# A two-layer decoder trunk on one core: preparing a pair's first blocks earlier, and the order of copies and casts at a turn of runs

## The chip, the cores and the metric

The kernel runs on one core of one Trainium2 chip. The metric is the device time of one execution in microseconds, as the median of three runs. The engines are TensorE (PE in the profile, with its weight loads as PEld), VectorE (DVE), ScalarE (ACT), GpSimd (POOL) and SyncE (SP), which issues the weight loads from memory.

## The reference

Two layers over 256 positions, model width 2048, feed-forward width 8192. Each layer is a mixer (a gated short convolution in the first layer, latent attention in the second) and a squared-ReLU MLP, each followed by a layer norm of 2^0.5 times the input plus the result:

```python
def sq_relu_mlp(x, w1, w2):
    return jnp.square(jax.nn.relu(x @ w1)) @ w2

for layer in range(DEPTH):            # DEPTH = 2
    mix = short_conv_mixer(...) if layer < N_A else mla_mixer(...)
    h = layer_norm(ALPHA * h + mix, ln_g[layer, 0], ln_b[layer, 0])
    h = layer_norm(ALPHA * h + sq_relu_mlp(h, mlp_w1[layer], mlp_w2[layer]),
                   ln_g[layer, 1], ln_b[layer, 1])
```

All of it is in float32. The change touches the two MLPs only.

## The kernel before

**Precision.** A float32 product is made of several products of a reduced format. Every weight block is split into a high part and a remainder: `split` (L144, L145) casts on ScalarE (`hi`) and subtracts on VectorE (`lo = raw - hi`). TensorE then multiplies high by high, low by high and high by low.

**The stream of weights.** All weights are read in the order of use, in a list `stream` of entries. An entry of kind "unit" is 128x1024 elements, one raw load (L165), one cast and one subtraction. A chunk of W1 (128 columns of the hidden layer) is two units. An entry of kind "plain" or "fast" is a *pair*: the rows of W2 for 256 hidden columns and 1024 output columns (one of two blocks, b = 0 or 1), two raw loads.

**Pairs.** A plain pair is multiplied with eight block products (`PLAINS`), 24 matmuls of 512 columns. A fast pair goes by the Strassen-Winograd scheme with seven (`FAST`), 21 matmuls: each of seven forms adds the product of a combination of the activations (`forms`, L665 to L668) and one of the weights to one of seven running sums in PSUM, numbered 1 to 7. The weight combinations are made from the raw blocks in place. `prepare` does it in three steps, with a `yield` between:

1. load both raw tiles; split the first (`hi`, `lo`: blocks 11 and 22); three subtractions in place (L193), of which each needs the one before;
2. split the result (`hi_t`, `lo_t`: combinations T1 and T2); a fourth subtraction; split that (the half-size `t`: T4);
3. split the second raw tile (`hi`, `lo`: block 21 and T3).

A plain pair has two steps, a unit one. Split blocks live in a pool of eight buffers (`WA`), raw tiles in one of six (`RAW`), T4 in one.

**Runs and turns.** `plan` lays out the MLP: runs of four pairs, alternately of block 0 and of block 1, with one W1 chunk after nearly every pair, so that TensorE works by turns on a chunk (L230, L234: `mm_like`) and on a group of seven or eight products (L295 to L297: `dot`). Runs of block 1 begin with a plain pair, the rest is fast; seven fast pairs and a plain one make a period. Only one block's sums fit into PSUM. At the end of a run (`turn`) ScalarE copies each sum out to SBUF (`spill`, L584) and the other block's sum back in (`seed`, L588), in the order of `FAST` or of the plain forms.

**Other work in the stage.** A finished chunk is evacuated by `whole` (L336 on ScalarE, L337 on VectorE). After every second one come ReLU (L722) and square (L658) on ScalarE, the activation forms on VectorE, and a split of the result (`hc`, `ha`). At the end of the runs `fold` (L614) and `combine` (L626, L627) turn the sums into the result.

**What sets the order.** The program is recorded in the order of the Python calls, and a scheduler then fixes the order on each engine at build time, by this order as priority and a cost model of its own; it also hands out the pools' buffers. On the chip each engine works through its list in that order. How early weights are prepared is set by `take`, which is called when a chunk or a group needs its entry: it first runs `prepare` steps up to eight steps past the start of that entry (`WA`), across the whole list in order of the stream.

Of the kernel before, what the change touches and what calls it, by code (L numbers as in the profile page):

```python
# [31 lines left out]
RAW, WA = 6, 8  # L32
# [7 lines left out]
GROUP = 3  # L40
# [8 lines left out]
def trunk(ctx: ExitStack, tc: tile.TileContext, xT, vecs, w_in, w_out, w_kv, w_q, w_uk, w_uv,  # L49
# [26 lines left out]
    stream = []  # L76
# [34 lines left out]
    size = {"unit": 1, "plain": 2, "fast": 3}  # L111
    start = [0]
# [3 lines left out]
    class Banks:  # L116
# [15 lines left out]
        @classmethod  # L132
        def next(cls):
            cls.count += 1
            if cls.only is not None:
                return cls.only
            return cls.more if cls.more is not None and cls.count % 8 >= 4 else pmm

    state = {"made": 0, "next": 0}
    ready = {}  # L140

    def split(hi, lo, src):

        nc.scalar.copy(hi, src)  # L144
        nc.vector.tensor_tensor(lo, src, hi.bitcast(F32), ALU.subtract)  # L145

    def tiled(w):
        return w.rearrange("p (b c) -> p b c", c=P)

    def parts(i):  # L150
        return tuple(whl.tile([P, 8, P], F32R, tag=t, name=f"{t}{i}") for t in ("hi", "lo"))
# [11 lines left out]
    def load_raw(i, src):  # L163
        raw = raws.tile([P, 1024], F32, tag="raw", name=f"raw{i}")
        nc.sync.dma_start(raw, src)  # L165
        return raw

    def prepare(i):

        kind, *src = stream[i]  # L170
        if kind == "unit":
            raw = load_raw(i, src[0])
            hi, lo = ready[i] = parts(i)
            split(hi, lo, tiled(raw))
            yield
            return
        r1, r2 = (load_raw(f"{i}_{j}", v) for j, v in enumerate(src))

        def finished(r, name):
            w = parts(f"{i}_{name}")  # L180
            split(*w, tiled(r))
            return [[v.rearrange("p b c -> p (b c)")[:, o:o + BW] for v in w] for o in (0, BW)]

        b11, b22, b21, b12 = r1[:, :BW], r1[:, BW:], r2[:, :BW], r2[:, BW:]
        out = {}
        if kind == "plain":
            out["11"], out["22"] = finished(r1, 1)
            yield
            out["21"], out["12"] = finished(r2, 2)
            ready[i] = out  # L190
            yield
            return
        minus = lambda o, x, y: nc.vector.tensor_tensor(o, x, y, ALU.subtract)  # L193
        out["11"], out["22"] = finished(r1, 1)
        minus(b11, b12, b11)
        minus(b12, b12, b22)
        minus(b22, b22, b11)
        yield
        out["T1"], out["T2"] = finished(r1, "t")
        minus(b11, b21, b22)  # L200
        f = state["fast"].tile([P, 2, BW], F32R, tag="t4", name=f"t4_{i}", bufs=1)
        split(f[:, 0, :], f[:, 1, :], b11)
        out["T4"] = [f[:, 0, :], f[:, 1, :]]
        yield
        out["21"], out["T3"] = finished(r2, 2)
        ready[i] = out
        yield

    def all_steps():
        for i in range(2 * GROUP, len(stream)):  # L210
            yield from prepare(i)

    making = all_steps()

    def take(n=2):

        i = state["next"]
        state["next"] += n
        while state["made"] < min(start[i] + WA, start[-1]):
            next(making)  # L220
            state["made"] += 1
        got = [ready.pop(i + j) for j in range(n)]
        return got

    def psum(name):
        return Banks.next().tile([P, 512], F32, tag="mm", name=name)
# [18 lines left out]
    def mm_like(ps, w, x, n=NC):  # L245

        for h in range(0, NC, n):
            for k in range(h, h + n):
                high(ps, w, k, x[k], k == 0)
            for k in range(h, h + n):  # L250
                low(ps, w, k, x[k], k == NC - 1)
# [22 lines left out]
    def group_of(n):  # L274

        return [(take(), psum("ps_g")) for _ in range(n)]

    def products(n, x, group=0, cuts=()):

        ws = group_of(group)  # L280
        at = [0, *cuts, NC]
        for k0, k1 in zip(at, at[1:]):
            if ws:
                mm_run(ws, x, k0, k1, NC, tiles_first=True)
        yield from [ps for _, ps in ws]
        for i in range(group, n):
            w = take()
            ps = psum("ps_u")
            mm_like(ps, w, x)
            yield ps  # L290
# [42 lines left out]
    def whole(ps, out):  # L333

        t = tmp.tile([P, T], F32, tag="evac", name="t")
        nc.scalar.copy(t, ps[:, T:])  # L336
        nc.vector.tensor_tensor(out, ps[:, :T], t, ALU.add)  # L337
# [174 lines left out]
    for half, cuts in enumerate(FIRST):  # L512
        pieces = [load(2 * u + half, first[:, GROUP * half + u, :], cuts) for u in range(GROUP)]
        for b0, b1 in zip(cuts, cuts[1:]):
            at = slice(8 * half + b0, 8 * half + b1)
# [4 lines left out]
                put_split(xhl[m], xres[:, m, :])  # L520
            for p in pieces:
                next(p)
    state["made"] = 2 * GROUP
    nc.sync.dma_start(vec, vecs)

    zt = array("b", F32R, "z", NC, 2 * T)
# [4 lines left out]
    for m in range(NC):  # L531
# [17 lines left out]
        if m >= NC // 2:  # L549
# [4 lines left out]
    summed(ln, products(NC, z), residual)  # L554

    FAST = (("1", "11", "11"), ("3", "S4", "22"), ("5", "S1", "T1"), ("6", "S2", "T2"),
            ("4", "22", "T4"), ("2", "12", "21"), ("7", "S3", "T3"))
    PLAINS = (("3", "12", "22"), ("1", "22", "22"), ("2", "11", "11"), ("4", "21", "11"),
              ("3", "11", "12"), ("1", "21", "12"), ("2", "12", "21"), ("4", "22", "21"))

# [77 lines left out]
    def mlp(idx, ln, hook, blocks, fast):  # L638
# [8 lines left out]
        def normal():  # L647
            k = next(todo, None)
            if k is not None:
                ln.normal(k, xhl[k])  # L650
# [3 lines left out]
        def pair():  # L654
            return fast.tile([P, 8 * P], F32, tag="sf", name="sf", bufs=2)

        def square(f):
            nc.scalar.activation(f[:, :4 * P], f[:, :4 * P], AF.Square)  # L658

        def forms(f):  # L660

            a21, a11, a12 = (f[:, i * P:(i + 1) * P] for i in (1, 0, 2))
            s1, s2, s4 = (f[:, i * P:(i + 1) * P] for i in (4, 6, 7))
            blocks = f.rearrange("p (a c) -> p a c", c=P)
            nc.vector.tensor_tensor(s1, a21, f[:, 3 * P:4 * P], ALU.add)  # L665
            nc.vector.tensor_tensor(blocks[:, 5:7, :], blocks[:, 1:5:3, :], a11.unsqueeze(1).to_broadcast([P, 2, P]),
                                    ALU.subtract)
            nc.vector.tensor_tensor(s4, a12, s2, ALU.subtract)  # L668
# [31 lines left out]
        def parts_of(j):  # L700

            i = j % 4
            if j >= 4:
                both = [(one[:, i, c * P:(c + 1) * P], two[:, i, c * P:(c + 1) * P]) for c in range(8)]
            else:
                both = [[t[:, i, (4 * o + c) * P:(4 * o + c + 1) * P] for o in range(2)] for t in (one, two) for c in range(4)]
            return dict(zip(NAMES, both))
# [4 lines left out]
        for at, step in enumerate(steps):  # L712
            if step[0] == "m":
                m = step[1]
                w, ps = take(), psum("ps_m")
                mm_like(ps, w, xhl, 8)
                if m % 2 == 0:
                    f = pair()
                half = f[:, m % 2 * T:(m % 2 + 1) * T]
                whole(ps, half)  # L720
                if m % 2:
                    nc.scalar.activation(f[:, :4 * P], f[:, :4 * P], AF.Relu)  # L722
                    square(f)
                    j, cols = m // 2, 4 * P
                    if j < KEPT:
                        forms(f)
                        cols = 8 * P
                    split(one[:, j % 4, :cols], two[:, j % 4, :cols], f[:, :cols])
                if m == FF // P - 3:
                    Banks.only = None  # L730
                continue
            _, b, j, plain, first, last = step
            w, = take(1)
            later = [s for s in steps[at + 1:] if s[0] == "group"]
            turns = plain and bool(later) and not later[0][3]
            sums.group(b, w, parts_of(j), plain, last, turns)
            if later:
                if last:
                    sums.turn(later[0][1], later[0][3])
                elif turns:  # L740
                    sums.spill("1")
                    sums.seed("1", (b, "1"))
            if first and j + 4 >= KEPT and b == 0 and j + 2 >= KEPT:
                folded = sums.fold(1)
            if not later:
                folded = sums.combine(0) + folded
            if count < 4:
                normal()
                normal()
            if hook is not None:  # L750
                hook(count)
            count += 1
# [37 lines left out]
    with tc.tile_pool(name="fast1", bufs=1) as fast:  # L790
        mlp(1, before, prepare_one, to_wide, fast)
# [250 lines left out]
    with tc.tile_pool(name="fast2", bufs=1) as fast:  # L1042
        mlp(3, after, None, to_out, fast)
# [86 lines left out]
```

## Time and profile before

| | |
|---|---|
| median of three runs | 2031.51 us (2030.67 to 2031.93) |
| the profiled execution | 2031.37 us |
| its span, first to last instruction | 2029.6 us |
| TensorE busy, matmuls | 2004.9 us (99%) |
| VectorE busy | 1729.8 us (85%) |
| ScalarE busy | 1384.2 us (68%) |
| DMA | 385.31 MB, 190 GB/s on average |
| granted TensorE clock | 0.999 |

The first copy of a sum (L584) starts at 423.5 us of the span, in the first layer's MLP, the last at 1935.3, in the second's; between the two MLPs lies the attention. Matmuls overlap one another, so the shown length of one is more than the time from one to the next: the busy share says that TensorE hardly rests, not how fast it works. In a row of groups the columns are line, engine, operation, tile written and tiles read, shapes, count, busy us, mean ns, idle us before them and what ended it. In a timeline a row has its start and length in us, and in brackets the idle time before it and what ended that.

### The profile page before, as it was taken

What the parts mean: (1) busy time and instruction counts of PE and PEld (TensorE: products, weight loads), DVE (VectorE), ACT (ScalarE), POOL (GpSimd) and SP (SyncE); (2) the same over time, 40 slices, a digit from 0 to 9 for tenths busy, and PEclk for the clock granted to TensorE, in tenths of its full rate; (3) what the DMA queues carried; (4) which work ended last, traced back from release to release, by engine and by line L of the source; (5) the groups of instructions that cost most, each with busy time, mean ns of one, the idle gap of its engine ahead of it and who ended that gap; (6) DMA issues with size and microseconds to landing.
All of it is one profiled execution on the core that took longest, in us unless ns stands there. A gap on an engine that the chain in (4) does not pass through costs nothing.

```text
span 2029.6 us, 29846 instructions
## 1 busy us (share of the span) xinstructions
PE 2004.9 (99%) x11088; PEld 1735.4 (86%) x11088; DVE 1729.8 (85%) x2575; ACT 1384.2 (68%) x2071; POOL 2.3 (0%) x21
## 2 busy tenths in 40 slices
PE   9999999999999999999999999999999999999997
PEld 8888888988888888888889998898888888888886
DVE  7667677799999999999988888779899999999996
ACT  6444445577877888777756655568777788787861
POOL 0000000000000000000000000000000000000000
PEclk9999999999999999999999999999999999999999
DMA  9665556455555565555654534655555556556672
GB/s 312 206 190 190 189 189 189 150 183 194 180 207 179 205 207 198 203 174 207 235 189 157 167 124 131 201 168 166 187 189 199 193 207 208 182 196 203 207 231 102
DMA packets 108002, 385.31 MB, mean 190 GB/s; under 512 B 11984, under 2 KB 13392, under 8 KB 107856
## 3 DMA queue, kind: packets, MB, share of 16 engines
q1 hardware_dynamic: 107712, 383.13, 56.6%
q8 instruction: 87, 1.43, 0.3%
q14 instruction: 59, 0.48, 0.1%
q10 hardware_dynamic: 144, 0.26, 0.0%
HBM read 381.25 MB, written 2.10 MB: 189 GB/s over the span
## 4 chain that ended last, share of the span: by engine, by line
PE 61%; DVE 17%; ACT 14%; issue 5%; DMA 2%; DVEq 0%; ACTq 0%; SPq 0%
PE ps_u L230 13%; PE ps_m L230 9%; PE ps_u L234 7%; DVE lo L145 7%; PE ps_m L234 5%; DVE raw L193 4%; ACT hi L144 4%; PE sum L296 3%; PE sum L297 3%; PE sum L295 3%; ACT sums L584 2%; ACT hi_t L144 2%; DVE lo_t L145 2%; ACT sum L588 2%; DMA raw<-in_w_dram 1%
## 5 line engine op out<-in xcount | busy, mean ns | idle before, releaser
L145 DVE TENSOR_TENSOR lo<-raw,hi 128x1024 fp32r<-128x1024 f32 x712 | 850.7, 1219 | 127.8 <-ACT hi L144 51.2
L144 ACT CAST hi<-raw 128x1024 fp32r<-128x1024 f32 x712 | 726.2, 1050 | 261.2 <-PE ps_u L230 158.1
L230 PE MATMUL ps_m<-xhl,hi 128*128 128x512 f32 x1792 | 449.3, 391 | 3.0 <-DVE sf L337 2.2
L230 PEld LDWEIGHTS ps_m<-xhl,hi 128*128 128x128 f32 x1792 | 328.6, 188 | 69.1 <-DVE sf L337 2.8
L234 PEld LDWEIGHTS ps_m<-xhl,lo 128*128 128x128 f32 x1792 | 244.3, 190 | 17.4
L234 PE MATMUL ps_m<-xhl,lo 128*128 128x256 f32 x1792 | 249.7, 282 | 0.0
L296 PE MATMUL sum<-lo,hc 128*128 128x512 f32 x512 | 202.9, 396 | 1.0 <-DVE lo L145 1.0
L295 PE MATMUL sum<-hi,hc 128*128 128x512 f32 x512 | 196.8, 396 | 5.2 <-ACT sum L588 5.1
L193 DVE TENSOR_TENSOR raw<-raw,raw 128x512 f32<-128x512 f32 x276 | 189.3, 686 | 3.0
L297 PE MATMUL sum<-hi,ha 128*128 128x512 f32 x448 | 175.1, 391 | 0.0
L144 ACT CAST hi_t<-raw 128x1024 fp32r<-128x1024 f32 x92 | 96.6, 1050 | 113.5 <-DVE raw L193 113.4
L230 PE MATMUL ps_u<-xhl_a,hi 128*128 128x512 f32 x720 | 172.0, 391 | 0.0
L145 DVE TENSOR_TENSOR lo_t<-raw,hi_t 128x1024 fp32r<-128x1024 f32 x92 | 112.7, 1225 | 68.5 <-ACT hi_t L144 68.5
L230 PEld LDWEIGHTS ps_u<-xhl_a,hi 128*128 128x128 f32 x720 | 132.4, 188 | 25.8
L584 ACT COPY sums<-sum 128x512 f32<-128x512 f32 x204 | 118.0, 583 | 43.3 <-PE sum L297 41.4
L295 PEld LDWEIGHTS sum<-hi,hc 128*128 128x128 f32 x512 | 95.6, 188 | 31.5 <-ACT sum L588 9.4
L296 PEld LDWEIGHTS sum<-lo,hc 128*128 128x128 f32 x512 | 96.5, 189 | 23.5 <-DVE lo L145 8.4
L588 ACT COPY sum<-sums 128x512 f32<-128x512 f32 x186 | 110.0, 593 | 2.7
L297 PEld LDWEIGHTS sum<-hi,ha 128*128 128x128 f32 x448 | 84.3, 188 | 15.9
L234 PEld LDWEIGHTS ps_u<-xhl_a,lo 128*128 128x128 f32 x720 | 92.3, 191 | 3.5
L234 PE MATMUL ps_u<-xhl_a,lo 128*128 128x256 f32 x720 | 93.4, 283 | 0.0
L722 ACT ACTIVATE sf<-sf 128x512 f32<-128x512 f32 x56 | 35.4, 631 | 57.2 <-DVE sf L337 57.2
(240 smaller groups left out, 3285.0 us busy)
## 6 DMA issues: line engine op xcount, KB each, us to landing
raw<-in_w_dram SPq DMA_DIRECT2D x288, 512.0 KB, 4.5
raw<-in_w2f_dram SPq DMA_DIRECT2D x224, 512.0 KB, 5.7
raw<-in_w_in_dram SPq DMA_DIRECT2D x90, 512.0 KB, 4.3
raw<-in_w_out_dram SPq DMA_DIRECT2D x32, 512.0 KB, 4.1
raw<-in_w_o_dram SPq DMA_DIRECT2D x32, 512.0 KB, 3.9
raw<-in_w_kv_dram SPq DMA_DIRECT2D x10, 512.0 KB, 4.3
raw<-in_w_q_dram SPq DMA_DIRECT2D x8, 512.0 KB, 4.0
raw<-in_w_uk_dram SPq DMA_DIRECT2D x8, 512.0 KB, 4.2
```

The source lines that it names most:

```text
L144: nc.scalar.copy(hi, src)
L145: nc.vector.tensor_tensor(lo, src, hi.bitcast(F32), ALU.subtract)
L193: minus = lambda o, x, y: nc.vector.tensor_tensor(o, x, y, ALU.subtract)
L230: nc.tensor.matmul(ps, w[blk // 8][0][:, blk % 8, :], x, start=first, stop=False)
L234: nc.tensor.matmul(ps[:, :T], w[blk // 8][1][:, blk % 8, :], x[:, :T], start=False, stop=last)
L295: nc.tensor.matmul(ps, x[0], w[0], start=first, stop=False, skip_group_check=goes_on)
L296: nc.tensor.matmul(ps, x[0], w[1], start=False, stop=False, skip_group_check=goes_on)
L297: nc.tensor.matmul(ps, x[1], w[0], start=False, stop=last, skip_group_check=goes_on)
L584: nc.scalar.copy(self.slot(self.live.pop(p)), self.bank[p])
L588: nc.scalar.copy(self.bank[p], self.at(key))
L722: nc.scalar.activation(f[:, :4 * P], f[:, :4 * P], AF.Relu)
```

## The change

Two things are moved; the amount of work stays the same.

First, the order in which entries are prepared is now a list of its own (`sequence`). Where two units (a W1 chunk) are followed by a fast pair, the pair's first step is put in front of the two units and its other steps behind them: pair, unit, unit, pair, pair. `make_up_to` works through this list with one generator per entry. The second and third step of a fast pair are divided differently: the second tile's split (21, T3) moves ahead of T4's, and T4 goes into the third step. The order of the forms is changed to match: the form that uses T4 (number 4) is now the last of the seven, in `group` as in `turn`.

Second, `take` has a second argument, how many steps to run ahead, and the last group of a run asks for five instead of eight. The steps that this leaves out are recorded after the turn, so behind the copies of the sums.

```diff
+        yield
+        out["21"], out["T3"] = finished(r2, 2)
         f = state["fast"].tile([P, 2, BW], F32R, tag="t4", name=f"t4_{i}", bufs=1)
         split(f[:, 0, :], f[:, 1, :], b11)
         out["T4"] = [f[:, 0, :], f[:, 1, :]]
-        yield
-        out["21"], out["T3"] = finished(r2, 2)
         ready[i] = out
         yield
 
-    def all_steps():
-        for i in range(2 * GROUP, len(stream)):
-            yield from prepare(i)
-
-    making = all_steps()
-
-    def take(n=2):
+    sequence, i = [], 2 * GROUP
+    while i < len(stream):
+        if [k for k, *_ in stream[i:i + 3]] == ["unit", "unit", "fast"]:
+            sequence += [i + 2, i, i + 1, i + 2, i + 2]
+            i += 3
+        else:
+            sequence += [i] * size[stream[i][0]]
+            i += 1
+    making = {}
+    last = {i: at for at, i in enumerate(sequence)}
+
+    def make_up_to(n):
+        while state["made"] < min(n, len(sequence)):
+            i = sequence[state["made"]]
+            state["made"] += 1
+            if i not in making:
+                making[i] = prepare(i)
+            next(making[i])
+
+    def take(n=2, ahead=None):
         i = state["next"]
         state["next"] += n
-        while state["made"] < min(start[i] + WA, start[-1]):
-            next(making)
-            state["made"] += 1
-        got = [ready.pop(i + j) for j in range(n)]
-        return got
+        mine = max(last.get(j, -1) + 1 for j in range(i, i + n))
+        make_up_to(max(mine, start[i] - 2 * GROUP + (WA if ahead is None else ahead)))
+        return [ready.pop(i + j) for j in range(n)]
...
     FAST = (("1", "11", "11"), ("3", "S4", "22"), ("5", "S1", "T1"), ("6", "S2", "T2"),
-            ("4", "22", "T4"), ("2", "12", "21"), ("7", "S3", "T3"))
+            ("2", "12", "21"), ("7", "S3", "T3"), ("4", "22", "T4"))
...
             _, b, j, plain, first, last = step
-            w, = take(1)
+            w, = take(1, 5 if last else None)
```

More of the change, by code (lines that the diff above doesn't have):

```diff
@@ L522, in trunk @@
                 next(p)
-    state["made"] = 2 * GROUP
     nc.sync.dma_start(vec, vecs)
```

## The prediction

> **What bounds the kernel.** I read the page's busy times first, then TensorE's groups of instructions, then the waits, then the timelines of TensorE, ScalarE and VectorE round one turn of runs. The page:
>
> ```profile
> span 2029.6 us, 29846 instructions
> PE 2004.9 (99%) x11088; PEld 1735.4 (86%) x11088; DVE 1729.8 (85%) x2575; ACT 1384.2 (68%) x2071; POOL 2.3 (0%) x21
> ```
>
> TensorE is shown busy for 99%, so the change can win only what TensorE waits. Its groups (count, busy us, mean ns, idle before) and one row of the waits:
>
> ```profile
> L230 PE MATMUL ps_m<-xhl,hi 128*128 128x512 f32 x1792 | 449.3, 391 | 3.0 <-DVE sf L337 2.2 <-ACT hi L144 0.8
> L296 PE MATMUL sum<-lo,hc 128*128 128x512 f32 x512 | 202.9, 396 | 1.0 <-DVE lo L145 1.0
> L295 PE MATMUL sum<-hi,hc 128*128 128x512 f32 x512 | 196.8, 396 | 5.2 <-ACT sum L588 5.1
> L295 PE MATMUL sum<-hi_t,hc 128*128 128x512 f32 x168 | 65.4, 389 | 0.0
> L296 PE MATMUL sum<-t,hc 128*128 128x512 f32 x92 | 36.8, 400 | 0.4 <-DVE t L145 0.3
> PE sum L295 <- ACT sum L588: 5.1, 10, 0.5
> ```
>
> An undisturbed 512-column matmul of the sums shows 389 ns; a mean of 396 is time lost inside the bars. The ceiling of the change: `hi` 5.2 + 512 x 0.007 = 8.8 us, `lo` 1.0 + 3.6 = 4.6, `t` 0.4 + 92 x 0.011 = 1.4 and as much again at most for its other rows, `ps_m` 3.0: about 18.5 us in both MLPs. The last row counts the places: ten waits for a sum's copy back into PSUM (L588).
>
> TensorE at one of the ten, a turn from a run of block 1 to a run of block 0, and the next such place:
>
> ```profile
> 531.54 1.98 PE L230 MATMUL ps_m<-xhl,hi 128*128 128x512 f32 x8
> 537.10 0.40 PE L295 MATMUL sum<-hi,hc 128*128 128x512 f32 x1
> 541.89 1.98 PE L230 MATMUL ps_m<-xhl,hi 128*128 128x512 f32 x8
> 547.45 0.40 PE L295 MATMUL sum<-hi,hc 128*128 128x512 f32 x1
> 551.18 0.73 PE L295 MATMUL sum<-hi,hc 128*128 128x512 f32 x2
> 552.42 0.50 PE L295 MATMUL sum<-hi,hc 128*128 128x512 f32 x1 [0.51 <-ACT sum L588]
> 552.98 0.40 PE L297 MATMUL sum<-hi,ha 128*128 128x512 f32 x1
> 637.69 0.50 PE L295 MATMUL sum<-hi,hc 128*128 128x512 f32 x1 [0.52 <-ACT sum L588]
> ```
>
> A W1 chunk takes 547.45 - 541.89 = 5.56 us, a fast group 541.89 - 537.10 = 4.79 (21 matmuls, 0.228 each), so a plain one 24 x 0.228 = 5.47. Eight chunks, seven fast groups and a plain one make 7 x 10.35 + 11.03 = 83.5 us; the two turns stand 85.3 apart. So 1.8 us are lost per period, and ten periods give 18, in line with the ceiling. Of it the turn has 1.2: from 547.45 to 552.98 there are 19 matmuls, 4.33 us of work in 5.53.
>
> **Why the turn waits.** ScalarE and VectorE in the same stretch:
>
> ```profile
> 527.34 0.36 ACT L336 COPY t<-ps_m 128x256 f32<-128x256 f32 x1
> 532.73 1.05 ACT L144 CAST hi_t<-raw 128x1024 fp32r<-128x1024 f32 x1 [5.03 <-DVE raw L193]
> 533.68 3.89 ACT L144 CAST hi<-raw 128x1024 fp32r<-128x1024 f32 x4
> 537.48 0.61 ACT L144 CAST t<-raw 128x512 fp32r<-128x512 f32 x1
> 538.26 0.58 ACT L584 COPY sums<-sum 128x512 f32<-128x512 f32 x1
> 541.22 0.64 ACT L722 ACTIVATE sf<-sf 128x512 f32<-128x512 f32 x1
> 541.76 0.59 ACT L588 COPY sum<-sums 128x512 f32<-128x512 f32 x1
> 542.27 0.63 ACT L658 ACTIVATE sf<-sf 128x512 f32<-128x512 f32 x1
> 543.27 1.06 ACT L144 CAST hi_t<-raw 128x1024 fp32r<-128x1024 f32 x1
> 551.77 0.59 ACT L588 COPY sum<-sums 128x512 f32<-128x512 f32 x1
> ```
>
> ```profile
> 530.23 0.42 DVE L337 TENSOR_TENSOR sf<-ps_m,t 128x256 f32<-128x256 f32 x1
> 530.56 1.40 DVE L193 TENSOR_TENSOR raw<-raw,raw 128x512 f32<-128x512 f32 x2
> 532.00 0.69 DVE L193 TENSOR_TENSOR raw<-raw 128x512 f32<-128x512 f32 x1
> 533.81 1.23 DVE L145 TENSOR_TENSOR lo_t<-raw,hi_t 128x1024 fp32r<-128x1024 f32 x1 [1.11 <-ACT hi_t L144]
> 540.70 0.42 DVE L337 TENSOR_TENSOR sf<-ps_m,t 128x256 f32<-128x256 f32 x1
> 544.36 1.23 DVE L145 TENSOR_TENSOR lo_t<-raw,hi_t 128x1024 fp32r<-128x1024 f32 x1 [0.21 <-ACT hi_t L144]
> 546.64 0.69 DVE L193 TENSOR_TENSOR raw<-raw,raw 128x512 f32<-128x512 f32 x1
> 547.24 1.22 DVE L145 TENSOR_TENSOR lo<-raw,hi 128x1024 fp32r<-128x1024 f32 x1
> 555.96 1.23 DVE L145 TENSOR_TENSOR lo_t<-raw,hi_t 128x1024 fp32r<-128x1024 f32 x1 [1.12 <-ACT hi_t L144]
> DVE lo_t L145 <- ACT hi_t L144: 5.6, 7, 1.1
> DVE lo L145 <- ACT hi L144: 0.6, 2, 0.3
> ACT hi L144 <- DMA raw<-in_w_dram: 0.2, 1, 0.2
> ```
>
> From 538.26 ScalarE works without a gap: fourteen copies of sums out and in, six casts between them. The copy back of sum 2 starts at 551.77, too late. It is late because ScalarE sat idle for 5.03 us ahead of 532.73, waiting for VectorE's three subtractions (L193), and then had its casts to make up. VectorE is behind: from `lo_t` to `lo_t` it takes 10.55 and 11.60 us, 11.1 on average, where TensorE takes 10.35 for chunk and group. It is late by its own chain: subtraction, subtraction, subtraction, cast on ScalarE, `lo_t`, where it waits for the cast 5.6 us in a period (the rows without a time, of the window 552.4 to 637.6).
>
> **The change, part by part.** No instruction is added or removed; only the MLPs' order moves. The built order of the changed program shows the following.
>
> *The chain is interleaved.* A fast pair's first step stands in front of the chunk's two units, so the two `lo` of the units, and often the evacuation L337, fall between its subtractions. A subtraction behind the one that it needs costs 0.72 (530.56 to 532.00 is 1.44 for two); with other work next it costs 0.60 (546.64 to 547.24). That saves 2 x 0.12 = 0.24 in a pair. L337 (0.33, 530.23 to 530.56) goes into the wait for the cast in the four pairs of seven whose wait is 1.1. So some 0.24 + 0.33 x 4/7 = 0.43 in a pair. In the plain stage the chain of the first fast pair moves in front of units whose casts VectorE now waits for: the 1.1 of that `lo_t`, the 0.6 of the second row and about 0.6 of L337 and the links go, 2.3 us. After the plain stage and two pairs VectorE is then 2.3 + 2 x 0.43 = 3.2 us earlier at the turn than now. The Trainium skill ("VectorE: DVE Perf Modes", "The DRAIN you can't avoid") says that the next operation waits for the pipe to empty whether or not a semaphore stands between, which would make interleaving worth nothing: the 0.24 would go and the lead would be some 0.5 us smaller. The trace disagrees, 0.72 against 0.60, and decides.
>
> *The turn.* In the built order ScalarE's queue from the first copy to the copy back of sum 2 is: ten copies at 0.51 (541.76 to 542.27), six casts at 0.95 (532.73 to 533.68), the half cast and an evacuation 0.78 (537.48 to 538.26), two activations at 0.54 (541.22 to 541.76), together 12.7 us, where it was 14.1 (538.26 to 552.36). Sum 4, two copies, goes last. So it is done at 550.9 if ScalarE never waits. TensorE, with form 4 moved to the end, wants sum 2 after 14 matmuls, at 547.45 + 14 x 0.228 = 550.6. That is a wait of 0.3. The order has a new wait in it: the first activation (L722) is now second in the queue, due at 538.7, and needs L337, which now stands behind two more subtractions: 540.70 + 1.2 - 3.2 = 538.7 to its start, 539.1 to its end. It holds the queue for 0.3: the turn's wait is 0.6 instead of 1.2. Ten turns: -6 us. Sum 6, wanted at 549.5, is back at about 548.9, and sum 4 at about 555, when it is wanted; both are covered by less than 1 us.
>
> *The rest.* 18.5 - 12 = 6.5 us are waits for `lo` and `t` late in the seven fast groups, in the first turns, and for L337 ahead of `ps_m` at the runs' end (2.2 us of the 3.0). All are VectorE's lateness; a lead of 2 to 3 us should take most of the small ones and part of the large one. I take 4 of 6.5: nothing would go if the lead were used up, 6.5 if not.
>
> Nothing outside the MLPs moves. On SyncE's queue a pair's two raw loads are now issued ahead of the chunk's two; the same four loads a pair go into six buffers. In that window they land so:
>
> ```profile
> raw<-in_w2f_dram SPq DMA_DIRECT2D x16, 512.0 KB, 5.8
> ```
>
> A unit's buffer comes free at its `lo` and is wanted by a cast one pair later; of the 10.35 us some 2 lie between cast and `lo`, 5.8 are the landing, and about 2.5 are left. Now ScalarE waits 0.2 for raw loads in a period. I cost them at nothing; if that slack were gone, the cast would wait for the excess in every pair.
>
> Sum: -6 - 4 = -10 us. The profiled execution took 2031.37 (span 2029.6 and 1.8 round it), the median is 2031.51: **2021.5 us**. 0.2% is 4 us, about what a measurement can tell from no change.
>
> **Rivals.** *The queue blocks (slower).* ScalarE's order at the turn puts L722, and `hi_t` with the cast `hc`, ahead of the copy back of sum 3; now three copies out and two back come before the activation. If VectorE's lead is not 3.2 but 1.6, the queue stands 1.6 longer and the turn waits 2.2: +1.0 at each of ten, +10 us, and 2041.5 if the rest stays. It decides from a lead under 2.6 (wait over 1.2). For it: 5.03 us of idleness ahead of 532.73 with four casts ready behind. Against it: seven waits of VectorE for `hi_t` that can be seen to shrink. The Trainium skill ("TensorE: Matmul & The Clock Gate", "Architectural detail") calls ScalarE's queue strictly first-in first-out; by that rule a copy cannot pass a waiting cast, and the 5.03 us agree. *It all goes.* With a lead over 3.5 the turn waits 0.3 or less and the rest goes too: -9 - 6.5 = -15.5, 2016. *The wait only moves (no change).* The copies were meant to stand ahead of the next pair's casts, but in the built order six casts still lie between them, as now; with a lead of 2.6 the turn waits as now and the small ones go or return elsewhere: within 3 us of 2031.
>
> **Chances.** Forecast 0.50, all goes 0.18, only moved 0.14, blocked 0.18. Faster by over 0.2%: 0.68; within: 0.14; slower: 0.18. The range goes from the ceiling with a margin (2031.5 - 18.5 = 2013, less 1) to the worst half of the blocked case left out: 2012 to 2037.
>
> **What would show it.** Right: `ACT hi_t <- DVE raw` and `DVE lo_t <- ACT hi_t` shrink; `PE sum L295 <- ACT sum` falls below 5.1; the same turns stand 84.3 us apart; VectorE's `lo` waits on TensorE go. Wrong: L722 or `hi_t` at the turn shows idle time over 1 us with sum copies behind it, and TensorE's waits move to sums 6 or 2 and grow; or ScalarE waits for the raw loads.

## The result, and the profile after

The changed kernel takes 2022.06 us in the median of four runs (2019.17 to 2023.98), the kernel before 2031.72 beside it: a ratio of 0.9952, with an interval from 0.9934 to 0.9969. Timed once more on another occasion (e0 below, five runs): 2019.59, 0.9949 (0.9936 to 0.9961). The forecast was 2021.5. The profiled execution took 2019.17, its span 2017.4. Its page:

```profile
span 2017.4 us, 29774 instructions
PE 1994.7 (99%) x11088; PEld 1737.5 (86%) x11088; DVE 1715.3 (85%) x2575; ACT 1381.1 (68%) x2071; POOL 2.3 (0%) x21
```

TensorE's busy share says as little as before. Its groups in the changed kernel (its lines stand 11 to 13 lower: L307 to L309 are the products of the sums, L242 and L246 the chunk's, L595 and L599 the copies out and back, L348 and L349 the evacuation, L733 the ReLU), and then the rows of its waits (waiting engine and line, releaser: us in total, times, longest):

```profile
L242 PE MATMUL ps_m<-xhl,hi 128*128 128x512 f32 x1792 | 449.3, 391 | 2.3 <-DVE sf L349 2.1
L308 PE MATMUL sum<-lo,hc 128*128 128x512 f32 x512 | 200.4, 391 | 0.0
L307 PE MATMUL sum<-hi,hc 128*128 128x512 f32 x512 | 202.0, 395 | 4.8 <-ACT sum L599 4.8
```

```profile
ACT t L348 <- PE ps_m L246: 89.1, 43, 4.7
DVE lo_t L145 <- ACT hi_t L144: 63.4, 72, 1.3
ACT hi_t L144 <- DVE raw L193: 55.5, 26, 3.8
ACT hi L144 <- DMA raw<-in_w_dram: 19.4, 25, 2.4
PE sum L307 <- ACT sum L599: 5.2, 6, 1.9
```

The waits for `lo` are gone: no idle time in the second row, and a mean of 391 instead of 396. The waits for a sum's copy come to 5.2 us, as before (5.1), but at six places instead of ten. The same whole-run rows of the kernel before, for the two engines that prepare the weights:

```profile
ACT hi_t L144 <- DVE raw L193: 113.4, 64, 5.0
DVE lo_t L145 <- ACT hi_t L144: 68.5, 86, 1.1
ACT hi L144 <- DMA raw<-in_w_dram: 16.0, 16, 3.4
ACT t L336 <- PE ps_m L234: 12.6, 4, 4.0
```

The last row against the 89.1 of above says that ScalarE now waits for TensorE, at 43 places: there the preparation is ahead. It is a sign and no measure of the gain, for in the experiment e1 below the same row has 19.0 and the time is the same. ScalarE's waits for VectorE's subtractions are halved. VectorE's waits for the cast `hi_t` hardly shrink.

The turn of runs that the prediction showed, in the timelines of the changed kernel: TensorE, with the same place one period later, and then ScalarE.

```profile
547.19 0.40 PE L307 MATMUL sum<-hi,hc 128*128 128x512 f32 x1
550.16 0.39 PE L308 MATMUL sum<-lo,hc 128*128 128x512 f32 x1
550.58 0.50 PE L307 MATMUL sum<-hi,hc 128*128 128x512 f32 x1
634.26 0.50 PE L307 MATMUL sum<-hi,hc 128*128 128x512 f32 x1
```

```profile
537.04 0.37 ACT L348 COPY t<-ps_m 128x256 f32<-128x256 f32 x1 [2.79 <-PE ps_m L246]
537.74 0.59 ACT L595 COPY sums<-sum 128x512 f32<-128x512 f32 x1 [0.32 <-PE sum L309]
538.40 0.63 ACT L733 ACTIVATE sf<-sf 128x512 f32<-128x512 f32 x1
549.92 0.61 ACT L599 COPY sum<-sums 128x512 f32<-128x512 f32 x1
```

Ahead of this turn ScalarE was idle for 5.03 us in the kernel before, waiting for VectorE; now it is idle for 2.79, waiting for TensorE: it has caught up. Sum 2 is back at 550.53, 12.8 us behind the first copy. TensorE comes to it at 550.58, 0.42 behind the matmul ahead, where 0.23 is undisturbed. The two turns stand 83.7 us apart; they stood 85.3 apart, and 83.5 is the ideal.

In the second MLP a wait is new. It stands at the turns to the plain group, which come about 42 us, half a period, behind such a turn. TensorE and ScalarE at one of them:

```profile
1540.90 0.50 PE L307 MATMUL sum<-hi,hc 128*128 128x512 f32 x1 [0.92 <-ACT sum L599]
```

```profile
1534.04 1.05 ACT L144 CAST hi<-raw 128x1024 fp32r<-128x1024 f32 x1 [1.04 <-DMA raw<-in_w_dram]
1540.26 0.59 ACT L599 COPY sum<-sums 128x512 f32<-128x512 f32 x1
```

A cast waits 1.04 us for a raw load, with copies of sums behind it in ScalarE's queue, and the copy that TensorE needs ends at 1540.85.

Summed over the MLPs' matmuls, by how far each start-to-start time exceeds the median of its shape, TensorE lost 13.7 and 14.4 us in the two MLPs before (28.1), 5.6 and 11.5 after (17.1). Of the 10.9 us of gain (from values before rounding), 8.9 come from the ten turns to a run of fast groups (12.4 us before, 3.5 after). The five turns to a plain group in the second MLP cost 6.7 instead of about 1.1. The other places, the waits for `lo` and the ends of the runs above all, lost 7.6 us less. The span is 12.2 us shorter; the rest of that, 1.3, lies in the first 50 us, where nothing was changed.

### The profile page after: what moved, and what is told of

Read it like the earlier page. It is cut to its first block, busy times and chain, and to the rows that moved or that the text cites. A ratio compares the mean times of both kernels' runs of the same rounds, so it can differ in the third digit from the quotient of the medians.

```text
span 2017.4 us, 29774 instructions
## 1 busy us (share of the span) xinstructions
PE 1994.7 (99%) x11088; PEld 1737.5 (86%) x11088; DVE 1715.3 (85%) x2575; ACT 1381.1 (68%) x2071; POOL 2.3 (0%) x21
## 4 chain that ended last, share of the span: by engine, by line
PE 82%; DVE 9%; ACT 4%; issue 2%; DMA 2%; DVEq 0%; ACTq 0%; SPq 0%
PE ps_m L242 16%; PE ps_u L242 13%; PE ps_m L246 8%; PE ps_u L246 7%; PE sum L307 7%; PE sum L308 7%; PE sum L309 7%; DVE lo L145 3%; DVE raw L193 2%; PE ps_d L309 1%; PE ps_d L308 1%; PE ps_d L307 1%; DMA raw<-in_w_dram 1%; ACT hi L144 1%; PE ps_w L282 1%
## 5 line engine op out<-in xcount | busy, mean ns | idle before, releaser
L144 ACT CAST hi<-raw 128x1024 fp32r<-128x1024 f32 x712 | 735.4, 1052 | 273.5 <-PE ps_u L242 158.1
L242 PE MATMUL ps_m<-xhl,hi 128*128 128x512 f32 x1792 | 449.3, 391 | 2.3 <-DVE sf L349 2.1
L242 PEld LDWEIGHTS ps_m<-xhl,hi 128*128 128x128 f32 x1792 | 328.4, 188 | 68.2 <-DVE sf L349 3.9
L246 PEld LDWEIGHTS ps_m<-xhl,lo 128*128 128x128 f32 x1792 | 245.2, 190 | 17.9
L246 PE MATMUL ps_m<-xhl,lo 128*128 128x256 f32 x1792 | 250.8, 282 | 0.0
L307 PE MATMUL sum<-hi,hc 128*128 128x512 f32 x512 | 202.0, 395 | 4.8 <-ACT sum L599 4.8
L193 DVE TENSOR_TENSOR raw<-raw,raw 128x512 f32<-128x512 f32 x276 | 189.0, 685 | 1.3
L309 PE MATMUL sum<-hi,ha 128*128 128x512 f32 x448 | 173.9, 390 | 0.0
L242 PE MATMUL ps_u<-xhl_a,hi 128*128 128x512 f32 x720 | 171.9, 391 | 0.0
L145 DVE TENSOR_TENSOR lo_t<-raw,hi_t 128x1024 fp32r<-128x1024 f32 x92 | 112.6, 1224 | 63.4 <-ACT hi_t L144 63.4
L242 PEld LDWEIGHTS ps_u<-xhl_a,hi 128*128 128x128 f32 x720 | 132.4, 188 | 25.7
L595 ACT COPY sums<-sum 128x512 f32<-128x512 f32 x204 | 118.4, 587 | 32.6 <-PE sum L309 31.9
L144 ACT CAST hi_t<-raw 128x1024 fp32r<-128x1024 f32 x92 | 96.6, 1050 | 56.1 <-DVE raw L193 55.5
L307 PEld LDWEIGHTS sum<-hi,hc 128*128 128x128 f32 x512 | 96.4, 188 | 27.7 <-ACT sum L599 10.2
L599 ACT COPY sum<-sums 128x512 f32<-128x512 f32 x186 | 110.9, 596 | 1.3
L348 ACT COPY t<-ps_m 128x256 f32<-128x256 f32 x112 | 41.7, 372 | 89.1 <-PE ps_m L246 89.1
L309 PEld LDWEIGHTS sum<-hi,ha 128*128 128x128 f32 x448 | 84.2, 188 | 17.6
L246 PEld LDWEIGHTS ps_u<-xhl_a,lo 128*128 128x128 f32 x720 | 92.3, 191 | 3.5
L246 PE MATMUL ps_u<-xhl_a,lo 128*128 128x256 f32 x720 | 93.4, 283 | 0.0
```

The costliest lines, as they stand in the source:

```text
L242: nc.tensor.matmul(ps, w[blk // 8][0][:, blk % 8, :], x, start=first, stop=False)
L246: nc.tensor.matmul(ps[:, :T], w[blk // 8][1][:, blk % 8, :], x[:, :T], start=False, stop=last)
L307: nc.tensor.matmul(ps, x[0], w[0], start=first, stop=False, skip_group_check=goes_on)
L309: nc.tensor.matmul(ps, x[1], w[0], start=False, stop=last, skip_group_check=goes_on)
L595: nc.scalar.copy(self.slot(self.live.pop(p)), self.bank[p])
L599: nc.scalar.copy(self.bank[p], self.at(key))
```

## The experiments

All were timed over four to eleven runs. Loss is TensorE's in the two MLPs, summed as above; "dependent" counts subtractions (L193) with another right behind, of which the second waits for the first; the last two columns are the total waits of VectorE for `hi_t` and of ScalarE for raw chunk loads. e6 and e11 make other combinations of the weights than the scheme needs; they serve as measurements only.

| kernel | us | ratio to before (interval) | loss | dependent | lo_t on hi_t | hi on raw |
|---|---|---|---|---|---|---|
| before | 2029.8 to 2031.7 | 1 | 13.7 + 14.4 | 148 | 68.5 | 16.0 |
| e0: changed, again | 2019.59 | 0.9949 (0.9936 to 0.9961) | 5.9 + 10.1 | 5 | 63.5 | 16.8 |
| e1: sequence alone | 2019.42 | 0.9943 (0.9929 to 0.9956) | 8.0 + 7.8 | 23 | 48.0 | 26.3 |
| e2: turn alone | 2044.61 | 1.0070 (1.0057 to 1.0082) | 19.7 + 20.4 | 148 | 71.5 | 13.8 |
| e3: old forms | 2020.48 | 0.9952 (0.9939 to 0.9964) | 8.2 + 8.7 | 5 | 62.8 | 21.8 |
| e4: 7 raw buffers | 2012.60 | 0.9914 (0.9900 to 0.9928) | 3.7 + 5.3 | 17 | 53.3 | 1.5 |
| e5: 5 raw buffers | 2026.26 | 0.9983 (0.9974 to 0.9992) | 13.3 + 11.4 | 20 | 41.6 | 113.2 |
| e6: free chain | 2022.89 | 0.9958 (0.9946 to 0.9971) | 9.5 + 7.7 | 0 | 54.3 | 9.4 |
| e7: turn in one MLP | 2016.05 | 0.9930 (0.9918 to 0.9943) | 5.6 + 9.5 | 11 | 56.2 | 21.5 |
| e8: chain between units | 2034.80 | 1.0020 (1.0011 to 1.0029) | 15.0 + 15.2 | 26 | 94.2 | 19.7 |
| e9: before, 7 raw buffers | 2032.84 | 1.0017 (1.0008 to 1.0025) | 13.3 + 14.7 | 136 | 71.9 | 7.7 |
| e10: e1, 7 raw buffers | 2012.06 | 0.9911 (0.9898 to 0.9925) | 4.7 + 3.1 | 18 | 50.0 | 1.9 |
| e11: before, cast covered | 2011.56 | 0.9909 (0.9892 to 0.9925) | 3.5 + 4.1 | 123 | 27.4 | 5.5 |

### Which part does it

The changed kernel again, and its two parts apart.

> The changed kernel once more, to have its time on the same chip as its parts. Theory (both parts are needed: the interleaved chain brings VectorE, and with it ScalarE, forward; the later steps at a turn shorten what stands ahead of the copies): 2022 again, 9 to 10 us below the kernel before, within 2 us. A spread of 4 us between its executions (2019.2 to 2024.0 so far) would speak for something that varies by itself, the raw loads: then ScalarE's waits for raw loads differ between this profile and the first, and TensorE's waits for sums in the second MLP with them.

```diff
 e1 (of the changed kernel)
-            w, = take(1, 5 if last else None)
+            w, = take(1)
```

> The new order of preparation and of the forms alone; the last group of a run asks for eight steps again, not five. Theory A (the chain and VectorE's lead do it; the turn's part is small): ScalarE still waits for TensorE ahead of a turn's first copy, so it starts as early as in the changed kernel. Its queue from the first copy to the end of the copies has nine casts at 0.95 instead of eight, 17.5 us instead of 16.6; sum 4 comes back 0.9 later, where the changed kernel had it back 0.3 us ahead of its use. So up to 0.6 at each of ten turns: 2022 to 2028, and 2025 if half of it shows. Rival B (the copies ahead of the casts at the turn do it): without them the waits of sum L307 for ACT sum stay at 5 us or more at the turns to block 0 and the time goes back to 2030. Rival C (the order of steps does everything): 2022.

```diff
 e2 (of the kernel before)
-    def take(n=2):
+    def take(n=2, ahead=WA):
-        while state["made"] < min(start[i] + WA, start[-1]):
+        while state["made"] < min(start[i] + ahead, start[-1]):
-            w, = take(1)
+            w, = take(1, 5 if last else WA)
```

> The kernel before, with one thing changed: the last group of a run asks for five steps instead of eight. Theory A: in the built order sums 6, 4 and 2 come back 1.0, 1.4 and 1.2 us sooner behind a turn's first copy, but sum 7 at the same 14.2 us, and VectorE's chain is as late as before: ScalarE still sits idle some 5 us ahead of the turn's casts for DVE raw, the TensorE wait goes from sum 2 to sum 7, and the time is 2028 to 2031. Rival B (the turn's order is what counts): each turn to block 0 loses its 1.2 us, 2020 to 2022.

The changed kernel came out 11.2 us below the kernel before, somewhat more than expected; the waits in its second MLP came again, 0.5 to 1.2 us each, and so did the spread of some 5 us between its executions. The order of preparation alone (with the order of the forms) gives all of the gain: rival C, with 2019.4 even below its 2022. So the theory that both parts are needed falls. The turn's part alone makes the kernel slower by 14 us, which neither theory expected. Its trace at the turn that was shown, and the row of the waits:

```profile
552.41 0.73 PE L295 MATMUL sum<-hi,hc 128*128 128x512 f32 x2
553.67 0.50 PE L296 MATMUL sum<-lo,hc 128*128 128x512 f32 x1 [0.53 <-DVE lo L145]
```

```profile
PE sum L296 <- DVE lo L145: 13.0, 22, 1.2
```

The wait for the sum's copy is indeed gone there (552.42 had 0.51 of it), but the steps that were put off are then late themselves: two waits for `lo` per period in its place. Here, where VectorE has no lead, preparing less far ahead moves the wait to the weights and makes it longer (13.0 us against 5.1).

Why the turn's part is not needed with a lead is seen in e1's trace. ScalarE's queue at the turn is longer than in the changed kernel, as expected, with the last sum back at 641.85, but the built order has put its matmuls late as well:

```profile
636.91 1.99 PE L242 MATMUL ps_m<-xhl,hi 128*128 128x512 f32 x8
639.00 0.50 PE L307 MATMUL sum<-hi,hc 128*128 128x512 f32 x1
```

After five forms TensorE goes on to the next chunk and does the products of a late sum among its matmuls. (The kernel before does so too: behind the wait at 552.42 it has three matmuls of the chunk and then goes back to a sum.) The order of the products within a group is not fixed by the forms' list: the scheduler moves those of late sums.

### The order of the forms

```diff
 e3 (of the changed kernel): T4 again in the second step, and
-            ("2", "12", "21"), ("7", "S3", "T3"), ("4", "22", "T4"))
+            ("4", "22", "T4"), ("2", "12", "21"), ("7", "S3", "T3"))
```

> The changed kernel, with T4 in the second step again and form 4 fifth of the seven, in the groups as at the turns. Theory A (the lead is what counts; the form order only says which sum is late): VectorE's lead is the same, so ScalarE waits for TensorE as in the changed kernel (ACT t on PE ps_m near 89 us), and the time is 2022 to 2025; the last copy back is due 14.2 to 16.1 us behind the first, where the changed kernel has 16.1. Rival B (T4 last is what gives the chain its slack): the waits of TensorE for DVE t and lo come back at 2 us or more, and the time is 2027 or more.

2020.5 against 2019.6, with overlapping intervals: theory A, though below its range, and ScalarE's waits for TensorE are 58.8 us and not near 89. No wait for `t` or `lo` came back. What is left of the change as the cause is the place of a pair's first step; no run leaves out the turn's part and the order of the forms together.

### The raw loads

The prediction gave them no price. One buffer more, one less, and one more in the kernel before:

```diff
 e4 (of the changed kernel; the room comes from temporaries outside the MLPs' pairs)
-RAW, WA = 6, 8
+RAW, WA = 7, 8
 e5 (of the changed kernel)
+RAW, WA = 5, 8
 e9 (of the kernel before, as e4)
+RAW, WA = 7, 8
```

> The changed kernel with a seventh raw buffer (the room is taken from temporaries of the layer norms and the attention, which share buffers more). Theory D (raw loads: ScalarE's waits for DMA raw, 19.4 and 2.4 us in the changed kernel, hold its queue at the turns of the second MLP, where TensorE waits 0.8 to 2.0 us for a sum at six places): these waits of ScalarE fall below 8 us, the six places shrink by half or more, and the time is 2015 to 2018. Rival E (the queue's own length at that turn makes the wait): the places stay at 0.7 or more each and the time is 2019 to 2022. The scheduler orders the turns of the first MLP a little differently with this buffer, which may move either by 1 us.

> The changed kernel with five raw buffers instead of six. The prediction gave a raw load some 2.5 us of slack and no price; with a seventh buffer ScalarE's waits for DMA raw fell from 22 to 1.5 us and the time by 7. Theory D (a buffer's time is what limits: with one less each load is issued about one cast and one subtraction later, 2 to 3 us, in each of 92 pairs): the slack is gone everywhere, ScalarE's waits for DMA raw go to 60 us or more, and the time is 2035 to 2060. Rival E' (the seventh buffer helped by the order that the scheduler made with it, not by the loads): 2019 to 2024.

> The kernel before with a seventh raw buffer (room as in the run of the changed kernel with seven). In the built order ScalarE's queue at the turns to block 0 is the same as in the kernel before, 14.2 us to the last copy back. Theory D' (raw loads became a limit only when the change moved a pair's loads ahead of the chunk's and the preparation ran earlier; in the kernel before VectorE's chain is the limit): 2028 to 2031, with the ten waits for a sum at the turns in place. Rival H (raw loads limited both alike): as much as the changed kernel won by it, 7 us: 2022 to 2025.

Rows of the waits, first of e4, then of e5, then of e9:

```profile
ACT hi L144 <- DMA raw<-in_w_dram: 1.5, 3, 0.7
```

```profile
ACT hi L144 <- DMA raw<-in_w_dram: 113.2, 97, 3.6
PE sum L307 <- ACT sum L599: 6.4, 13, 1.2
```

```profile
ACT hi L144 <- DMA raw<-in_w_dram: 7.7, 9, 2.4
PE sum L295 <- ACT sum L588: 5.2, 10, 0.5
```

With seven buffers ScalarE's waits for loads vanish, the turns to a plain group in the second MLP fall to 0.1 us each, though ScalarE's order there is the same as in the changed kernel from the first copy back on, and 7 us go: theory D, by more than it expected. TensorE's order of the products differs a little there, so that the order has a share is not excluded by e4 alone; e1 and e10 (below) are the same pair without the turn's part, and 7 us go again. With five the waits grow to some 1.2 us at 97 places, but TensorE loses only 7 us more: between D and its rival; most of these waits cost TensorE nothing. The kernel before gains nothing from the seventh buffer (it is 3 us slower, a little outside the range of D'); in the MLPs its loss is the same 28 us, with its ten waits in place. So loads became a limit only through the change: in the runs of pairs (430 to 990 and 1450 to 1937 us of the span) ScalarE's waits for loads were 1.5 us before and are 16.5 after, 0.7 in e4.

It is not that a load takes longer. The lists of DMA issues (count, size, median us from issue to landing) show the W2 loads before, after, and in e4:

```profile
raw<-in_w2f_dram SPq DMA_DIRECT2D x224, 512.0 KB, 5.7
```

```profile
raw<-in_w2f_dram SPq DMA_DIRECT2D x224, 512.0 KB, 4.1
```

```profile
raw<-in_w2f_dram SPq DMA_DIRECT2D x224, 512.0 KB, 4.0
```

The change made them land sooner, and the chunk loads (in_w) no later: 4.5 before, 4.4 after. What the seventh buffer changes is how long before its cast a chunk's load is issued: 10.0 us in the median in e4, 7.4 in the changed kernel. SyncE issues a load when VectorE has freed a raw buffer (in the changed kernel it waits 1075 us in all for `lo`); which tile holds its buffer too long in the changed kernel no run isolates.

### The turn's part, one MLP at a time, and with enough buffers

```diff
 e7 (of the changed kernel)
-            w, = take(1, 5 if last else None)
+            w, = take(1, 5 if last and idx == 1 else None)
 e10: e4 and e1 together
```

> The changed kernel, with five steps ahead at the last group of a run in the first MLP only, eight in the second. By the traces the first MLP went better with five (from 490 to 1065 us it took 574.0, with eight 576.7), the second with eight (two traces: from 1131 to the end 886.2, with eight 883.6). If these are the order's and not chance: 2016.5 to 2018, some 2.6 us below the changed kernel on the same chip. If chance: 2019 to 2020.5.

> The changed kernel with seven raw buffers and eight steps ahead everywhere: the order of preparation and of the forms, without the turn's part. Theory C' (the turn's five steps win nothing by themselves; what they still do is to keep raw loads apart): 2011 to 2014, the same as with them. Rival B' (once loads no longer hold ScalarE, the copies ahead of the casts count): 2 us or more above the run with five steps, 2015 to 2018.

e7 is 3.5 us below the changed kernel; its interval (to 0.9943) and that of the changed kernel (from 0.9936) overlap a little, and its profiled loss in the second MLP (9.5) is not as low as e1's (7.8), so the gain isn't settled as the order's. The profiled losses do point one way: in the first MLP 5.6 to 5.9 us in the three profiles with five steps there and 8.0 in e1, in the second 10.1 and 11.5 with five and 7.8 and 9.5 with eight. With seven buffers it doesn't matter (theory C'): e10, without the turn's part, takes 2012.06 and e4, with it, 2012.60. These two are the fastest that keep the scheme's combinations, 0.9% below the kernel before. No run shows a gain of the turn's part that is clear of its interval.

### What it is in the chain

The prediction gave two gains to the interleaving: subtractions that no longer stand right behind the one that they need, and other work inside the wait for the cast `hi_t`. Three kernels part them. e8 puts the chain's start between the chunk's units. e6 and e11 keep the preparation order of before, with other operands.

```diff
 e8 (of e1)
-            sequence += [i + 2, i, i + 1, i + 2, i + 2]
+            sequence += [i, i + 2, i + 1, i + 2, i + 2]
 e6 (of the kernel before): the second is independent, the third still makes hi_t wait
-        minus(b11, b12, b11)
-        minus(b12, b12, b22)
-        minus(b22, b22, b11)
+        minus(b12, b12, b11)
+        minus(b21, b21, b22)
+        minus(b11, b12, b11)
 e11 (of the kernel before): each needs the one before, hi_t only the first two
+        minus(b11, b12, b11)
+        minus(b22, b22, b11)
+        minus(b12, b12, b22)
```

> Eight steps ahead everywhere, and the pair's first step between the two units of the chunk instead of in front of both: unit, pair, unit, pair, pair. Theory A (what helps is that other work lies between the subtractions and between them and hi_t): one unit's lo is left to lie between, so half of the gain: 2023 to 2028, with half as many adjacent subtractions as the kernel before. Rival F (any place ahead of the second unit does): 2019 to 2021. Rival G (the chain must start ahead of both units, since the time at which it starts is what counts): 2029 to 2032.

> The kernel before, with its order of preparation, but the operands of the three subtractions (L193) are others: the second needs nothing of the first, the third, which still writes what hi_t reads, needs the first alone. So the combinations of the weights are not those that the scheme needs; the amount of work is the same. Theory A' (the price of a subtraction right behind the one that it waits for, 0.718 instead of 0.602 us at 148 places, 17 us of VectorE's time, is what keeps VectorE behind): VectorE gains some 0.2 us a pair of the 0.7 that it lacks, and the time is 2023 to 2028. Rival C' (only the place counts: the chain starts ahead of the two units, not between them and hi_t): 2029 to 2032.

> The kernel before, with its order of preparation and, as before, three subtractions of which each needs the one before, but the third writes the second raw tile instead of the first. What hi_t reads is then ready after the second, and the third lies beside the cast. The combinations of the weights are not those that the scheme needs; the amount of work is the same. Theory L (what VectorE loses is the sum of the subtractions' waits for each other and of the waits for hi_t behind them, whichever of the two is cut): in the kernel before 48 of the lo_t stand right behind the third subtraction and wait 53.5 us there; 0.6 of each goes, some 29 us, about twice what the waits of the subtractions for each other come to (17), which stay for the most part. So at least as much as the run that took those away: 2019 to 2025. Rival A' (only the price of a dependent subtraction counts): 2029 to 2032.

e8 has only 26 dependent subtractions left and is slower than the kernel before. VectorE's timeline at one pair, and the row of its waits:

```profile
541.60 0.68 DVE L193 TENSOR_TENSOR raw<-raw,raw 128x512 f32<-128x512 f32 x1
542.20 0.41 DVE L349 TENSOR_TENSOR sf<-ps_m,t 128x256 f32<-128x256 f32 x1
542.53 0.68 DVE L193 TENSOR_TENSOR raw<-raw 128x512 f32<-128x512 f32 x1
545.03 1.23 DVE L145 TENSOR_TENSOR lo_t<-raw,hi_t 128x1024 fp32r<-128x1024 f32 x1 [1.82 <-ACT hi_t L144]
```

```profile
DVE lo_t L145 <- ACT hi_t L144: 94.2, 74, 1.8
```

Other work lies between the subtractions, but `lo_t` comes right behind the third (in 72 of 92 pairs, 48 in the kernel before, 16 in the changed one), and VectorE stands still while ScalarE casts. The time lies nearest to rival G, by which the start of the chain is what counts; but e6 and e11 leave the start where the kernel before has it, and both gain. e6 takes the waits between subtractions away and 14 us of the waits for `hi_t` with them, and reaches four fifths of the change's gain in the old order (A'), though its subtractions now wait 21.8 us for W2 loads. e11 does the opposite: 123 dependent subtractions stay, but the third now lies beside the cast (VectorE's timeline, then the waits):

```profile
529.97 0.69 DVE L193 TENSOR_TENSOR raw<-raw 128x512 f32<-128x512 f32 x1
530.69 0.69 DVE L193 TENSOR_TENSOR raw<-raw,raw 128x512 f32<-128x512 f32 x1
531.78 1.23 DVE L145 TENSOR_TENSOR lo_t<-raw,hi_t 128x1024 fp32r<-128x1024 f32 x1 [0.39 <-ACT hi_t L144]
```

```profile
DVE lo_t L145 <- ACT hi_t L144: 27.4, 72, 0.5
ACT hi L144 <- DMA raw<-in_w_dram: 5.5, 7, 1.7
```

A wait of 1.1 becomes 0.4, 41 us of VectorE's waits are gone, and the time is 2011.56: below what theory L expected, nearly twice the change's gain, with six raw buffers and without the new order. So the wait for the cast behind the chain is the larger of the two prices in the kernel before, and rival A' (only the dependent subtraction counts) falls. e6 and e11 leave the scheduler to find its own order for the new operands, so the split between the two prices isn't exact. In the changed kernel it is open: its dependent subtractions are gone, but its waits for `hi_t` fell by 5 us only.

## Why the prediction came out right, step by step

**The cause.** Right. The waits at the turns come from VectorE's chain of three subtractions, cast and `lo_t`; e6 and e11 cut that chain by itself and TensorE's loss falls from 28 us to 17 and 8. The ceiling of 18.5 us was too low: by the times from start to start the MLPs lost 28.1, and e10 and e11 take back some 20 of it.

**The chain's term.** Right in sign, wrong in its parts. The price of a dependent subtraction was 0.72 against 0.60: over the whole trace the medians are 0.718 at 148 places and 0.602 elsewhere, and in the changed kernel 5 such places are left. That is 143 x 0.116 = 16.6 us of VectorE's time, 0.18 in a pair where the prediction had 0.24 (it counted two in each pair, there were 1.6). The Trainium skill ("VectorE: DVE Perf Modes", "The DRAIN you can't avoid") measured eight copies to take as long with a semaphore after each as with one after the last; it also says: "A next op that is not held starts earlier". For these subtractions the traces show a price of the wait and an earlier start without it: e6 has 98 places with two side by side of which the second does not wait for the first, 0.602 in the median from start to start, where one is shown to last 0.68. The second half, the evacuation inside the wait for `hi_t`, did happen (51 of the `lo_t` now stand behind L349), but the sum of these waits fell only from 68.5 to 63.4, where 0.33 in four of seven of the 92 pairs had promised 17. So the sum of these waits was no measure of the gain. Nor are ScalarE's waits for TensorE: 89.1 us here, 19.0 in e1 at the same time, 34.9 in e10 and 56.1 in e4, which are faster, and 19.1 in e9, which gained nothing.

**The lead at the turn.** It was put at 3.2 us, less 1.2 for two more subtractions ahead of L337, so L337 at 538.7. L349 starts at 537.95, 2.75 earlier than before, with TensorE itself 0.26 earlier; it could have come half a us sooner at most, since the chunk had only just ended (ScalarE's 2.79 above, and its evacuation ends at 537.41). In the prediction's terms, with the two subtractions ahead of it, the lead was 540.70 + 1.2 - 537.95 = 4.0 us. The ReLU L733, second in the queue, had no wait at all, so the 0.3 that the prediction added for it did not come.

**The turn's term.** The number is nearly right, the reason is not. The queue to sum 2 took 12.8 us (12.7 forecast), and TensorE came to it after 14 matmuls, as forecast, with a wait of 0.2; ten turns gave 8.9 us instead of 6. But the prediction took the saving from the shorter queue, and that was not needed: e1 has a longer queue and the same time, e2 has the turn's part alone and takes 14 us more. The step that failed is to hold TensorE's order fixed, with sum 2 wanted after 14 matmuls whatever the queue: in e1 the scheduler places the products of late sums into the next chunk.

**The rest.** 4 us of 6.5 had been forecast; 7.6 went. The waits for `lo` and the 2.2 us at the end of the runs are gone; at the first turn of the first MLP 1.7 us are lost, by L349, where 0.8 were before.

**The raw loads.** "Cost nothing" was wrong by up to 7 us. The 2.5 us of slack allowed 5.8 for the landing; the loads land in 4.1 and 4.4 in the median, so by that sum the slack should have grown. The term that failed is the time from issue to cast. The sum has 10.35 - 2 = 8.3 us; in the runs of pairs a chunk's load has 7.4 in the median and less than 6.0 in a quarter of the cases (7.5 and 6.4 before). So a few casts wait, up to 2.4 us, with copies of sums behind them, and the seventh buffer ends it. One of the prediction's signs of being wrong, that ScalarE waits for the raw loads, did appear; and of its signs of being right, TensorE's waits for a sum's copy did not fall below 5.1, because the turns to the plain group brought new ones. The price of the loads and the larger gains cancelled: -8.9, -7.6 and +5.6 make -10.9 in the MLPs, against the forecast -10. That the number is so close is luck.

**The rivals.** "The queue blocks" was to decide from a lead under 2.6. The lead was 4.0, and the queue did not block at the turn that the prediction watched; its mechanism, a waiting cast with copies behind it, appeared all the same, at the other turn and behind a load. "The wait only moves" is what e2 and e8 show. "It all goes" was put at a lead over 3.5, which was there; what was missing is the seventh buffer.

## What to carry to other kernels

When two engines hand a tile to and fro, look for the operation that comes right behind the hand-over and waits for it: putting independent work there, or letting the hand-over start one step earlier, can be worth far more than it looks: one subtraction moved beside the cast won 18 us here (e11). Recording work later at a turn moved the wait and lengthened it where VectorE had no lead (e2), and with a lead it won nothing clear of noise. A change that brings preparation forward can make the loads' buffers the limit, though no load takes longer, so price the buffers with it, and test one buffer more and one less.

Left open: e11's order of the subtractions could, by the algebra, be had with the scheme's own combinations, since T3 = b12 - b22 equals b11 - T2, so T1 and T2 need only two. It needs the raw blocks laid out otherwise, and was not tried.

## What the hardware showed that was not expected

A 128x512 float32 subtraction on VectorE followed by one that waits for it takes 0.718 us from start to start (median), without a wait 0.602, though both run on the same engine in order. The same 512 KB load of W2 takes 5.7 us (median) from issue to landing in the kernel before and 4.1 in the changed one, with the same number of loads, and 4.0 with one more buffer; what makes the difference no run here tells. And a faster landing did not mean fewer waits: ScalarE's waits for loads grew in the kernel whose loads landed sooner.
